# Layer A of a two-layer encoder trunk: tokens transposed before their norm, and the second half of the queries made tile by tile

## The chip, the cores and the metric

One core of a Trainium2 chip runs the whole kernel in one launch. The metric is device time in microseconds (us) of one execution; lower is better. Inputs and output are float32.

## The reference, cut to what matters

The input x has 512 tokens of 1024 values. There are two residual layers, A and B, each followed by an MLP with a squared ReLU. The change lies in layer A, the sparse attention:

```
xn = x * rsqrt(mean(x * x) + EPS) * g_attn_a
q, k, v, qi, ki, wi = split(xn @ w_in)          # 1024, 256, 256, 512, 64, 8 columns
q, k, qi, ki = rope(q), rope(k), rope(qi), rope(ki)
wi = wi * (8 ** -0.5 * 64 ** -0.5)
score[t, s] = sum_h relu(qi[t, h] . ki[s]) * wi[t, h]   # allowed keys only
keep the 128 best keys of each query
o = softmax(q . k / 8 over the kept keys) @ v     # 16 heads, 4 key heads
h = x + o @ w_o
```

The rotation (rope) multiplies pairs of columns by cos and sin of the position, so it is linear in its input; v and wi are linear in xn as well.

## The kernel before, in words

Tokens are worked on in four tiles t of 128. A product in float32 is made of three matmuls: each operand is split into a high part (a cast, on ACT) and a low part (the rest, on DVE or by a POOL-issued accumulating DMA), and high*high, high*low and low*high are added up in a PSUM bank (mm3). wunit loads a piece of weights (raw) and makes its two parts (whi, wlo).

A planner sets the order. The body only records operations; schedule (L237) then simulates the five queues with a cost per operation, gives each operation a due time from the sum of PE costs before it in program order, and picks for each engine the most urgent one that is ready and whose tiles have room. emit writes the instructions out in that order, and on the chip each engine runs its own list strictly in that order. Nearly all instructions therefore carry the helper's line, L416, in the profile, and are told apart by the names of their tiles. Tiles live in slots by size: 41 slots of 1024 words per partition (L423). Weight pieces may be fetched up to 40 us of PE cost ahead, and split up to 30 us ahead (L422). PSUM has 8 banks.

Layer A runs so. x is loaded by tiles (L601). rstd (L562) makes the norm factor r of a tile: two Square pieces on ACT with a sum, then small steps on DVE and ACT. The gain g_attn_a is loaded as one row (grow, L607) and spread over 128 partitions by two float32 matmuls of a row of ones (tile g). norm_T (L584) makes y = x * r * g on DVE, transposes y on PE (tile yT) and splits the result into xT. The planner has 20 transposes of the identity (tile warm) at the start of PE's list.

Then come the products with pieces of w_in: for every tile t, 264 columns (idx2: part of qi, ki, wi) and 320 columns (idx1: the rest of qi), with the index scores (tile ix) behind them; then keys and values by tokprod (kvdone, L736); then the queries in two halves hb of 512 columns. tokprod (L527) in order "k" takes one weight piece for all four tiles before the next piece, with four banks open. After each product, rope (L636) does three multiplications on DVE with the tables cosT and sinT and an add on POOL, and for queries stacks (L658) transposes the result (tile qT) and splits it into the stacks qs[t][hb].

The attention takes tile t after tile t, and for each of the four key heads: products lg of queries and keys, a sum with the mask on DVE, exp on ACT, scaling on POOL, transposes pT, and products pv. Key heads 0 and 1 use the first half of the queries, 2 and 3 the second. topk(t) makes the mask of tile t on DVE, in 16 rounds; topk(1) is recorded before tile 0, topk(2) and topk(3) behind tiles 0 and 1. The output projection (products tp on oT) follows, then the MLP, which begins with the products up. A later helper, column (L1008), loads the gains of layer B, gq and gkv, with a transposing DMA of single values.

Of the kernel before, what the change touches and what calls it, by code (L numbers as in the profile page):

```python
# [429 lines left out]
def body(ctx, tc, a, out):  # L430
# [25 lines left out]
    def const(shape, name):  # L456
        return rec.tile(VPool(rcst, name, 1), shape, F32, name)
# [10 lines left out]
    def bank(shape, name):  # L468
        return rec.tile(p_ps, shape, F32, name, quotas.get(name))
# [27 lines left out]
    def lows(stage):  # L497
        lo_eng[0] = G if stage in CFG["dl"] else V
# [58 lines left out]
    def gain(row):  # L557
        g = rec.tile(p_bt, [128, D], F32, "g")
        SP.dma_start(g, bass.AP(tensor=row.tensor, offset=row.offset, ap=[[0, 128], [1, D]]))
        return g  # L560

    def rstd(src, cuts=(0, 512, D)):  # L562
        n = len(cuts) - 1
        ss = small(n, "ss")
        for i in range(n):
            c = slice(cuts[i], cuts[i + 1])
            S.activation(scr([128, cuts[i + 1] - cuts[i]], "junk"), src[:, c], AF.Square, accum_out=ss[:, i:i + 1])
        v = small(4, "v")
        for i in range(1, n):
            V.tensor_tensor(v[:, 0:1], v[:, 0:1] if i > 1 else ss[:, 0:1], ss[:, i:i + 1], op=OP.add)  # L570
        V.tensor_scalar(v[:, 0:1], v[:, 0:1], 1.0 / D, EPS, op0=OP.mult, op1=OP.add)
        S.activation(v[:, 1:2], v[:, 0:1], AF.Ln)
        S.activation(v[:, 1:2], v[:, 1:2], AF.Exp, scale=-0.5)
        V.scalar_tensor_tensor(v[:, 2:3], v[:, 1:2], v[:, 0:1], v[:, 1:2], op0=OP.mult, op1=OP.mult)
        V.tensor_scalar(v[:, 2:3], v[:, 2:3], -0.5, 1.5, op0=OP.mult, op1=OP.add)
        r = small(1, "r")
        V.tensor_tensor(r, v[:, 1:2], v[:, 2:3], op=OP.mult)
        return r
# [5 lines left out]
    def norm_T(src, r, g, xT, t):  # L584
        for i in range(2):
            y = scr([128, 512], "y")
            c = slice(512 * i, 512 * i + 512)
            gc = g[i] if isinstance(g, list) else g[:, c]
            V.scalar_tensor_tensor(y, src[:, c], r, gc, op0=OP.mult, op1=OP.mult)
            b = bank([128, 4, 128], "yT")  # L590
            for k in range(4):
                PE.transpose(b[:, k, :], y[:, 128 * k:128 * k + 128], ident)
            c = slice(128 * t, 128 * t + 128)
            for k in range(2):
                split(xT[0][2 * i + k][:, :, c], xT[1][2 * i + k][:, :, c], b[:, 2 * k:2 * k + 2, :])

    def xl(xT):
        return lambda k, t: tuple(x[k // 2][:, k % 2, 128 * t:128 * t + 128] for x in xT)
# [5 lines left out]
        return x  # L604

    xt = [xload(0)]
    grow = const([1, D], "grow")  # L607
    SP.dma_start(grow, a["g_attn_a"][0:1])
    ones = const([1, 128], "ones")
    V.memset(ones, 1.0)  # L610
    g = [bank([128, 512], "g") for _ in range(2)]
    for i in range(2):
        PE.matmul(g[i], ones, grow[:, 512 * i:512 * i + 512], start=True, stop=True)

    wb = bank([128, 128], "warm")
    for _ in range(CFG["warm"]):
        PE.transpose(wb, ident, ident)

    w_in = a["w_in_a"][0]
    xT = new_xT()  # L620
    norm_T(xt[0], rstd(xt[0]), g, xT, 0)
    lows("i2")
    ui2 = [wN(w_in, 256 * j, 1856, 264) for j in range(4)]
    xt.append(xload(1))
    norm_T(xt[1], rstd(xt[1]), g, xT, 1)
    SP.dma_start(cosT, a["cos"].rearrange("(t p) d -> p t d", p=128))
    SP.dma_start(sinT, a["sin"].rearrange("(t p) d -> p t d", p=128))
    lows("i1")
    ui1 = [wN(w_in, 256 * j, 1536, 320) for j in range(4)]
    lows("a")  # L630
    for t in (2, 3):
        xt.append(xload(t))
        norm_T(xt[t], rstd(xt[t]), g, xT, t)
    SP.dma_start(bfc, a["b_f"].rearrange("(h o) -> h o", o=1))

    def rope(dst, src, t, nh, dup=None):  # L636
# [36 lines left out]
    def idx2(t, b):  # L673
        q = scr([128, 512], "qr")
        qr[t] = q
        if t:
            S.activation(wi[:, t, :], b[:, 256:264], AF.Copy, scale=float(8 ** -0.5 * 64 ** -0.5))
        k2 = scr([128, 1, 2, 64], "k2")
        if t:
            rope(q[:, 0:192].heads(64), b[:, 0:192].heads(64), t, 3)  # L680
        rope(q[:, None, 192:256], b[:, None, 192:256], t, 1, dup=k2)
        kb = bank([128, 128], "kb")
        PE.transpose(kb, k2.flat(), ident)
        c = slice(128 * t, 128 * t + 128)
        split(kid[:, 0, c], kid[:, 1, c], kb)
# [50 lines left out]
    def kvdone(t, b):  # L736
        ka, k = scr([128, 4, 64], "ka"), scr([128, 4, 2, 64], "kr")
        rope(ka, b[:, 0:256].heads(64), t, 4, dup=k)
        for c, e in ((0, 64), (64, 320)):
            S.copy(vf[t][:, c:e], b[:, 256:256 + e - c])  # L740
        if vv is not None:
            v = vv[t // 2][:, t % 2]
            split(v[:, :, 0, :], v[:, :, 1, :], b[:, 256:512].heads(64))
        krs[t] = k

    tokprod(xl(xT), w_in, 0, 8, 1024, 512, kvdone)
# [4 lines left out]
        split(kd[n][:, 0, :], kd[n][:, 1, :], b.flat())  # L751

    qs = [[big([128, 2, 4, 128], "qs") for _ in range(2)] for _ in range(NT)]
    for hb in range(2):
        def qdone(t, b, hb=hb):
            q = scr([128, 512], "qr")
            rope(q.heads(64), b.heads(64), t, 8)
            stacks(qs[t][hb], q, 0.125)
        tokprod(xl(xT), w_in, 0, 8, 512 * hb, 512, qdone)


    def topk(t):
# [7 lines left out]

    oT = new_xT("oT")
    topk(1)
    for t in range(NT):
        n = 128 * (t + 1)
        for kv in range(4):
            st = small(4, "st")
            rc = small(4, "rc")
            Ps = []
            for h in range(4):
                b = bank([128, 512], "lg")  # L780
                for p in range(2):
                    PE.matmul(b[:, :n], qs[t][kv // 2][:, h % 2, 2 * (kv % 2) + h // 2, :], kd[kv][:, p, :n],
                              start=p == 0, stop=p == 1)
                l = scr([128, 512], "l")
                mn = small(1, "mn")
                V.tensor_tensor_reduce(out=l[:, :n], in0=b[:, :n], in1=masks[t], op0=OP.add, op1=OP.min,
                                       scale=-1.0, scalar=BIG, accum_out=mn)
                S.activation(l[:, :n], l[:, :n], AF.Exp, bias=mn, scale=-1.0, accum_out=st[:, h:h + 1])
                Ps.append(l)
            V.reciprocal(rc, st)  # L790
            for h in range(4):
                G.tensor_scalar(Ps[h][:, :n], Ps[h][:, :n], rc[:, h:h + 1], 0.0, op0=OP.mult, op1=OP.add)
            pt = []
            for j in range(t + 1):
                b = bank([128, 4, 128], "pT")
                for h in range(4):
                    PE.transpose(b[:, h, :], Ps[h][:, 128 * j:128 * j + 128], ident)
                if t in CFG["pvf"]:
                    pf = scr([128, 4, 128], "pf")
                    S.copy(pf, b)  # L800
                    pt.append(pf)
                else:
                    ph, pl = scr([128, 4, 128], "ph", F32R), scr([128, 4, 128], "pl", F32R)
                    split(ph, pl, b)
                    pt.append((ph, pl))
            c = slice(128 * t, 128 * t + 128)
            if t in CFG["pvf"]:

                o = bank([128, 2, 128], "pv")
                for e in (1, 0):  # L810
                    for j in range(t + 1):
                        PE.matmul(o if e else o[0:64], vf[j][:, 64 * kv + 64 - 64 * e:64 * kv + 128],
                                  pt[j][:, e:4:2, :], start=j == 0, stop=j == t)
            else:

                pv, u, o = bank([128, 4, 128], "pv"), scr([64, 4, 128], "u"), scr([128, 2, 128], "o")
                for j in range(t + 1):
                    for i in range(2):
                        PE.matmul(pv, vv[j // 2][:, j % 2, kv].flat(), pt[j][i], start=j + i == 0, stop=j == t and i == 1)
                S.copy(u, pv[64:128])  # L820
                for e in range(2):
                    V.tensor_tensor(o[64 * e:64 * e + 64], pv[0:64, e:4:2, :], u[:, e:4:2, :], op=OP.add)
            split(oT[0][kv][:, :, c], oT[1][kv][:, :, c], o)
        if t in (0, 1):
            topk(t + 2)
# [179 lines left out]


    hd = rec.tile(p_dr["hd"], [T, D], F32, "hd")
    def column(row, name):  # L1008

        g = const([128, 8], name)  # L1010
        SP.dma_start(g, row)
        return g

    gq = column(a["g_attn_b"][0].rearrange("(k p) -> p k", p=128), "gq")
    gkv = column(a["g_kv"].rearrange("(k p) -> p k", p=128), "gkv")
    xq, xk = new_xT(), new_xT()

    def afterA(t):
# [276 lines left out]
```

## Time and profile before

| | us |
|---|---|
| three runs | 1181.00 (median), 1179.83 to 1181.45 |
| the profiled execution: its own time | 1181.78 |
| the profiled execution: its span, first to last instruction | 1179.7 |
| PE busy in the span | 1154.7 (98%) |
| DVE, ACT, POOL busy | 773.3, 737.5, 235.4 |

The trace has one execution. PE is TensorE, DVE VectorE, ACT ScalarE, POOL GpSimd, SP the engine that issues most transfers; PEld is the weight load of PE. A stretch is counted in us from the start of the span. The granted clock (PEclk) is the share of TensorE's full speed that the throttle let through: 1.00 stands for 2.4 GHz, 0.50 for 1.2 GHz. A group's row gives the count, the busy time and the mean duration of one instruction in ns. Matmuls overlap, so the pace of a run of matmuls is its length divided by its count and not their mean duration.

### The profile page before, as it was taken

Reading aid. Unit: us, or ns where it says so; the run is one execution under the profiler, and the core shown is the slowest. Engines: PE = TensorE matmul, PEld = TensorE weight load, DVE = VectorE, ACT = ScalarE, POOL = GpSimd, SP = SyncE. Lnnn points to the kernel's source line nnn. Section 1 sums busy time; section 2 is a strip of 40 time slices with the busy share of each in tenths; the row PEclk is TensorE's granted clock in tenths of the full one; section 3 lists DMA queues with packets and bytes.
Section 4 is the critical chain, followed back from the end, with each engine's and each line's share of the span. In section 5 each row is a group of like instructions: output and inputs, shape, how many; then the busy total and the mean of one; then the engine's idle time right before and its main releaser. Section 6 shows DMA issues by size and latency. Waiting matters only on the chain. (4 is left out here: it accounts for less than half of the span.)

```text
span 1179.7 us, 16374 instructions
## 1 busy us (share of the span) xinstructions
PE 1154.7 (98%) x5688; PEld 959.0 (81%) x5688; DVE 773.3 (66%) x1474; ACT 737.5 (63%) x1385; POOL 235.4 (20%) x391
## 2 busy tenths in 40 slices
PE   8999899999999999999999999999999999999997
PEld 7878677888888888888897878888888888888885
DVE  6799979365735836658665458874558358366496
ACT  7751499955745745658584148997558456555562
POOL 0311344310110100200111058972101001002001
PEclk9999799999999999999999999999999999999999
DMA  9941620873791981965886313588638919729601
GB/s 296 223 90 63 206 55 19 179 176 129 191 272 39 247 248 57 248 215 140 235 199 143 108 37 108 167 209 175 160 113 214 250 56 234 244 71 244 220 18 72
DMA packets 147349, 187.85 MB, mean 159 GB/s; under 512 B 10162, under 2 KB 94130, under 8 KB 147267
## 3 DMA queue, kind: packets, MB, share of 16 engines
q1 hardware_dynamic: 131714, 130.18, 35.1%
q0 software_dynamic: 15552, 56.63, 24.8%
q8 instruction: 45, 0.74, 0.3%
q14 instruction: 38, 0.30, 0.1%
HBM read 125.94 MB, written 4.23 MB: 110 GB/s over the span
## 5 line engine op out<-in xcount | busy, mean ns | idle before, releaser
L416 PE MATMUL up<-xT,whi 128*128 128x512 f32 (+1 forms) x1152 | 323.4, 366 | 0.0
L416 PEld LDWEIGHTS up<-xT,whi 128*128 128x128 f32 x1152 | 207.9, 189 | 34.8
L416 POOL DMA_DIRECT2D wlo<-raw x108 | 95.3, 883 | 702.1 <-ACT wlo L416 291.7
L416 DVE TENSOR_TENSOR dlo<-raw,dhi 128x1024 fp32r<-128x1024 f32 x112 | 136.3, 1226 | 143.4 <-ACT dhi L416 89.3
L416 PE MATMUL up<-xT,wlo 128*128 128x512 f32 (+1 forms) x576 | 210.0, 366 | 0.0
L416 PE MATMUL tp<-dhi,xhi 128*128 128x512 f32 (+1 forms) x452 | 171.8, 389 | 1.2 <-DVE h L416 0.8
L416 PE MATMUL tp<-dlo,xhi 128*128 128x512 f32 (+1 forms) x452 | 171.5, 387 | 0.0
L416 PE MATMUL tp<-dhi,xlo 128*128 128x512 f32 (+1 forms) x452 | 170.8, 388 | 0.0
L416 ACT CAST whi<-raw 128x1024 fp32r<-128x1024 f32 (+2 forms) x124 | 124.2, 1025 | 74.2 <-DMA raw<-in_w_up_dram 66.3
L416 ACT CAST dhi<-raw 128x1024 fp32r<-128x1024 f32 x112 | 116.5, 1047 | 66.3 <-PE up L416 64.1
L416 ACT ACTIVATE wlo<-whi 128x1024 fp32r<-128x1024 f32 x108 | 112.7, 1061 | 23.9 <-DMA wlo<-raw 10.6
L416 PE MATMUL tp<-whi,xT 128*128 128x512 f32 (+2 forms) x432 | 123.5, 372 | 0.0
L416 PEld LDWEIGHTS up<-xT,wlo 128*128 128x128 f32 x576 | 108.4, 189 | 17.5
L416 DVE TENSOR_TENSOR h<-tp,h 128x512 f32<-128x512 f32 (+1 forms) x97 | 64.6, 681 | 80.8 <-PE tp L416 80.7
L416 PEld LDWEIGHTS tp<-dhi,xhi 128*128 128x128 f32 x452 | 84.8, 188 | 21.5 <-DVE h L416 1.4
L416 PEld LDWEIGHTS tp<-dhi,xlo 128*128 128x128 f32 x452 | 84.7, 188 | 17.4
L416 PEld LDWEIGHTS tp<-dlo,xhi 128*128 128x128 f32 x452 | 84.9, 188 | 16.9
L416 DVE TENSOR_TENSOR raw<-raw 128x1024 f32<-128x1024 f32 x64 | 76.6, 1220 | 19.3 <-DMA raw<-in_w_down_dram 18.7
L416 PEld LDWEIGHTS tp<-whi,xT 128*128 128x128 f32 x432 | 78.8, 192 | 12.2 <-ACT xT L416 0.2
L416 ACT ACTIVATE r<-up 128x512 f32<-128x512 f32 x64 | 37.9, 592 | 79.6 <-PE up L416 79.6
L416 ACT ACTIVATE l<-l,mn 128x128 f32<-128x128 f32 (+3 forms) x128 | 71.5, 563 | 22.4 <-DVE mn L416 22.0
L416 POOL TENSOR_SCALAR l<-l,rc 128x128 f32<-128x128 f32 (+3 forms) x128 | 69.1, 561 | 59.4 <-DVE rc L416 42.5
(178 smaller groups left out, 1939.6 us busy)
## 6 DMA issues: line engine op xcount, KB each, us to landing
wlo<-raw POOLq DMA_DIRECT2D x108, 512.0 KB, 8.6
raw<-in_w_down_dram SPq DMA_DIRECT2D x96, 512.0 KB, 11.5
raw<-in_w_up_dram SPq DMA_DIRECT2D x64, 512.0 KB, 6.7
raw<-in_w_kv_b_dram SPq DMA_DIRECT2D x16, 512.0 KB, 5.6
raw<-in_w_in_a_dram SPq DMA_DIRECT2D x12, 512.0 KB, 6.5
raw<-in_w_o_a_dram SPq DMA_DIRECT2D x8, 512.0 KB, 4.8
raw<-in_w_q_b_dram SPq DMA_DIRECT2D x8, 512.0 KB, 7.2
ck<-cd SPq DMA_DIRECT2D x16, 256.0 KB, 3.7
```

What stands on the lines that cost most here:

```text
L416: getattr(self.engs[o.eng], o.fn)(*a, **k)
```

## The change

The tokens are transposed as they are loaded. The gain g_attn_a becomes a column of 8 values per partition (column, now with a load of 8 rows, a transpose on PE and a copy on ACT), and is applied as the scale of the split into xT. The norm factor r is kept in a small table rs[t]; factor(t) multiplies it into the rows of cosT and sinT of that tile, so that the rotation applies it to queries and keys; values and the index weights wi take it as the scale of their copies. Tiles 0 and 1 are transposed each by itself, with splits 128 wide; tiles 2 and 3 together, 256 wide.

Both halves of the query weights are now recorded ahead of the query products. These run by token tile: first half for all tiles, second half of tile 0, then the second half of tile t + 1 at the head of attention tile t. The gains of layer B are loaded by the new column as well.

```diff
--- before.py
+++ after.py
@@ -559,6 +559,14 @@
         SP.dma_start(g, bass.AP(tensor=row.tensor, offset=row.offset, ap=[[0, 128], [1, D]]))
         return g
 
+    def column(g, name):
+
+        rows, b, c = const([8, 128], name + "r"), bank([128, 8], "gc"), const([128, 8], name)
+        SP.dma_start(rows, g.rearrange("(k p) -> k p", p=128))
+        PE.transpose(b, rows, ident[0:8, 0:8])
+        S.copy(c, b)
+        return c
+
     def rstd(src, cuts=(0, 512, D)):
         n = len(cuts) - 1
         ss = small(n, "ss")
@@ -585,8 +593,7 @@
         for i in range(2):
             y = scr([128, 512], "y")
             c = slice(512 * i, 512 * i + 512)
-            gc = g[i] if isinstance(g, list) else g[:, c]
-            V.scalar_tensor_tensor(y, src[:, c], r, gc, op0=OP.mult, op1=OP.mult)
+            V.scalar_tensor_tensor(y, src[:, c], r, g[:, c], op0=OP.mult, op1=OP.mult)
             b = bank([128, 4, 128], "yT")
             for k in range(4):
                 PE.transpose(b[:, k, :], y[:, 128 * k:128 * k + 128], ident)
@@ -604,33 +611,55 @@
         return x
 
     xt = [xload(0)]
-    grow = const([1, D], "grow")
-    SP.dma_start(grow, a["g_attn_a"][0:1])
-    ones = const([1, 128], "ones")
-    V.memset(ones, 1.0)
-    g = [bank([128, 512], "g") for _ in range(2)]
-    for i in range(2):
-        PE.matmul(g[i], ones, grow[:, 512 * i:512 * i + 512], start=True, stop=True)
+    ga = column(a["g_attn_a"][0], "ga")
 
     wb = bank([128, 128], "warm")
     for _ in range(CFG["warm"]):
         PE.transpose(wb, ident, ident)
 
+
+
     w_in = a["w_in_a"][0]
     xT = new_xT()
-    norm_T(xt[0], rstd(xt[0]), g, xT, 0)
+    rs = {}
+
+    def x_T(ts):
+        n = len(ts)
+        c = slice(128 * ts[0], 128 * ts[-1] + 128)
+        for k in range(0, 8, 4 // n):
+            b = bank([128, 4 // n, 128 * n], "yT")
+            for i in range(4 // n):
+                for u, t in enumerate(ts):
+                    PE.transpose(b[:, i, 128 * u:128 * u + 128], xt[t][:, 128 * (k + i):128 * (k + i) + 128], ident)
+            for i in range(k, k + 4 // n):
+                split(xT[0][i // 2][:, i % 2, c], xT[1][i // 2][:, i % 2, c], b[:, i - k, :], scale=ga[:, i:i + 1])
+
+    def factor(t):
+        r = const([128, 2], "ra%d" % t)
+        rr = rstd(xt[t])
+        V.tensor_copy(r[:, 0:1], rr)
+        V.tensor_scalar(r[:, 1:2], rr, float(8 ** -0.5 * 64 ** -0.5), None, op0=OP.mult)
+        rs[t] = r
+        V.tensor_scalar(cosT[:, t, :], cosT[:, t, :], r[:, 0:1], None, op0=OP.mult)
+        V.tensor_scalar(sinT[:, t, :], sinT[:, t, :], r[:, 0:1], None, op0=OP.mult)
+
+    x_T((0,))
     lows("i2")
     ui2 = [wN(w_in, 256 * j, 1856, 264) for j in range(4)]
     xt.append(xload(1))
-    norm_T(xt[1], rstd(xt[1]), g, xT, 1)
     SP.dma_start(cosT, a["cos"].rearrange("(t p) d -> p t d", p=128))
     SP.dma_start(sinT, a["sin"].rearrange("(t p) d -> p t d", p=128))
+    factor(0)
+    x_T((1,))
+    factor(1)
     lows("i1")
     ui1 = [wN(w_in, 256 * j, 1536, 320) for j in range(4)]
     lows("a")
     for t in (2, 3):
         xt.append(xload(t))
-        norm_T(xt[t], rstd(xt[t]), g, xT, t)
+    x_T((2, 3))
+    factor(2)
+    factor(3)
     SP.dma_start(bfc, a["b_f"].rearrange("(h o) -> h o", o=1))
 
     def rope(dst, src, t, nh, dup=None):
@@ -674,7 +703,7 @@
         q = scr([128, 512], "qr")
         qr[t] = q
         if t:
-            S.activation(wi[:, t, :], b[:, 256:264], AF.Copy, scale=float(8 ** -0.5 * 64 ** -0.5))
+            S.activation(wi[:, t, :], b[:, 256:264], AF.Copy, scale=rs[t][:, 1:2])
         k2 = scr([128, 1, 2, 64], "k2")
         if t:
             rope(q[:, 0:192].heads(64), b[:, 0:192].heads(64), t, 3)
@@ -737,10 +766,10 @@
         ka, k = scr([128, 4, 64], "ka"), scr([128, 4, 2, 64], "kr")
         rope(ka, b[:, 0:256].heads(64), t, 4, dup=k)
         for c, e in ((0, 64), (64, 320)):
-            S.copy(vf[t][:, c:e], b[:, 256:256 + e - c])
+            S.activation(vf[t][:, c:e], b[:, 256:256 + e - c], AF.Copy, scale=rs[t][:, 0:1])
         if vv is not None:
             v = vv[t // 2][:, t % 2]
-            split(v[:, :, 0, :], v[:, :, 1, :], b[:, 256:512].heads(64))
+            split(v[:, :, 0, :], v[:, :, 1, :], b[:, 256:512].heads(64), scale=rs[t][:, 0:1])
         krs[t] = k
 
     tokprod(xl(xT), w_in, 0, 8, 1024, 512, kvdone)
@@ -751,12 +780,23 @@
         split(kd[n][:, 0, :], kd[n][:, 1, :], b.flat())
 
     qs = [[big([128, 2, 4, 128], "qs") for _ in range(2)] for _ in range(NT)]
-    for hb in range(2):
-        def qdone(t, b, hb=hb):
+
+    def qdone(hb):
+        def done(t, b):
             q = scr([128, 512], "qr")
             rope(q.heads(64), b.heads(64), t, 8)
             stacks(qs[t][hb], q, 0.125)
-        tokprod(xl(xT), w_in, 0, 8, 512 * hb, 512, qdone)
+        return done
+    uq = [[wN(w_in, 256 * j, 512 * hb, 512) for j in range(4)] for hb in range(2)]
+
+    def qprod(hb, t):
+        b = bank([128, 512], "tp")
+        for k in range(8):
+            mm3(b, xl(xT)(k, t), tuple(u[:, k % 2, :] for u in uq[hb][k // 2]), k == 0, k == 7)
+        qdone(hb)(t, b)
+
+    for t in range(NT):
+        qprod(0, t)
 
 
     def topk(t):
@@ -770,8 +810,11 @@
 
     oT = new_xT("oT")
     topk(1)
+    qprod(1, 0)
     for t in range(NT):
         n = 128 * (t + 1)
+        if t + 1 < NT:
+            qprod(1, t + 1)
         for kv in range(4):
             st = small(4, "st")
             rc = small(4, "rc")
@@ -1005,14 +1048,8 @@
 
 
     hd = rec.tile(p_dr["hd"], [T, D], F32, "hd")
-    def column(row, name):
-
-        g = const([128, 8], name)
-        SP.dma_start(g, row)
-        return g
-
-    gq = column(a["g_attn_b"][0].rearrange("(k p) -> p k", p=128), "gq")
-    gkv = column(a["g_kv"].rearrange("(k p) -> p k", p=128), "gkv")
+    gq = column(a["g_attn_b"][0], "gq")
+    gkv = column(a["g_kv"], "gkv")
     xq, xk = new_xT(), new_xT()
 
     def afterA(t):
```

## Rows read from the trace of the kernel before

**Rows 1.** The page: span, and busy time, share and instructions of PE.

```profile
span 1179.7 us, 16374 instructions
PE 1154.7 (98%) x5688; PEld 959.0 (81%) x5688; DVE 773.3 (66%) x1474; ACT 737.5 (63%) x1385; POOL 235.4 (20%) x391
```

**Rows 2.** Stretches: PE, PEld, DVE, ACT, POOL busy (count); clock; DMA share, GB/s.

```profile
217.00:252.00 35.00, 35.00 (x164) 28.54 (x162) 14.91 (x38) 25.07 (x48) 7.52 (x9) 1.00 0.81 169
...
600.00:1179.70 579.70, 566.39 (x2778) 471.87 (x2776) 359.94 (x616) 353.69 (x654) 132.14 (x243) 0.99 0.57 151
```

**Rows 3.** Timeline of the start: start us, us, engine, what, count.

```profile
2.90 6.96 SPq L416 DMA_DIRECT2D raw<-in_w_in_a_dram  x8
...
12.02 0.63 ACT L416 CAST whi<-raw 128x528 fp32r<-128x528 f32 x1
...
12.86 0.74 PE L416 MATMUL tp<-whi,xT 128*128 128x264 f32 x2
...
16.51 2.56 DVE L416 TENSOR_TENSOR wlo<-raw,whi 128x528 fp32r<-128x528 f32 x4
...
16.75 0.54 PE L416 MATMUL tp<-whi,xT 128*128 128x320 f32 x1
```

**Rows 4.** Stretches of the start.

```profile
13.60:16.70 3.10, 1.24 (x8) 0.84 (x8) 3.10 (x10) 3.10 (x10) 0.00 (x0) 1.00 1.16 315
16.70:20.10 3.40, 3.37 (x15) 3.06 (x15) 3.40 (x7) 2.80 (x6) 0.00 (x0) 0.52 1.04 383
20.10:32.20 12.10, 11.91 (x89) 11.46 (x88) 10.05 (x29) 9.38 (x16) 3.82 (x6) 0.99 0.97 252
```

**Rows 5.** Forms, ACT and DVE to 60 us; last row ACT, 126 to 218.

```profile
L416 ACT CAST xT<-yT 128x256 fp32r<-128x256 f32 x16 | 5.6, 385 | 2.5 <-PE yT L416 1.9 <-DVE xT L416 0.6
L416 ACT ACTIVATE junk<-x 128x512 f32<-128x512 f32 x8 | 5.0, 622 | 3.3 <-DMA x<-in_x_dram 3.2
...
L416 ACT CAST kid<-kb 128x128 fp32r<-128x128 f32 x3 | 0.8, 272 | 0.0
...
L416 DVE TENSOR_TENSOR xT<-yT,xT 128x256 fp32r<-128x256 f32 x16 | 6.0, 418 | 1.4 <-ACT xT L416 1.4
L416 DVE SCALAR_TENSOR_TENSOR y<-x,r,g 128x512 f32<-128x512 f32 x8 | 5.9, 743 | 0.4 <-PE g L416 0.2
...
L416 DVE TENSOR_TENSOR kid<-kb,kid 128x128 fp32r<-128x128 f32 x3 | 0.9, 288 | 2.1 <-ACT kid L416 2.1
...
L416 ACT ACTIVATE l<-l,mn 128x128 f32<-128x128 f32 x16 | 6.4, 398 | 21.8 <-DVE mn L416 21.6
```

**Rows 6.** Stretches from the top-k to the end of the attention.

```profile
50.00:104.00 54.00, 53.51 (x245) 42.50 (x243) 53.51 (x154) 24.21 (x50) 8.12 (x10) 1.00 0.47 111
104.00:126.40 22.40, 22.13 (x104) 18.36 (x105) 21.88 (x48) 3.83 (x7) 2.77 (x3) 1.00 0.42 142
126.40:133.00 6.60, 3.69 (x28) 3.08 (x26) 6.55 (x22) 3.06 (x8) 5.04 (x4) 0.99 1.07 301
133.00:146.40 13.40, 11.79 (x46) 9.40 (x46) 11.64 (x47) 10.81 (x39) 4.28 (x13) 0.50 0.26 85
146.40:157.00 10.60, 10.42 (x58) 6.55 (x57) 9.63 (x41) 9.37 (x34) 5.09 (x12) 0.99 0.18 54
...
166.00:217.00 51.00, 50.74 (x278) 40.58 (x277) 42.96 (x115) 50.13 (x114) 23.57 (x37) 1.00 0.24 48
```

**Rows 7.** Waits, 126 to 147 us: who for whom, us, times, longest.

```profile
POOL qr L416 <- DVE rtmp L416: 20.7, 4, 19.7
...
PE qT L416 <- POOL qr L416: 3.0, 4, 1.0
```

**Rows 8.** DMA issues to 30 us: first weight pieces, count, KB, us to landing.

```profile
raw<-in_w_in_a_dram SPq DMA_DIRECT2D x4, 264.0 KB, 7.7
```

**Rows 9.** Stretches, PE's instructions on oT alone: busy (count), clock, DMA.

```profile
166.00:200.00 34.00, 6.92 (x18) 1.00 0.13 25
200.00:217.00 17.00, 9.86 (x31) 1.00 0.45 96
```

## The prediction

> **What bounds the kernel now.** I read the page first: PE is busy 1154.7 of 1179.7 us [rows 1]. With an engine at 98% nothing but PE's own lost time can be won, so I looked for where it is lost, in two forms: idle time, and time at a low granted clock, which the busy column hides. The view of busy time by stretch shows both. From 217 to 252 us, in the output projection, PE is never idle. After 600 us it is idle 579.7 - 566.4 = 13.3 us, in stages that the diff touches only with two small gain columns [rows 2]. So the question is what is lost before 217 us. There are two places.
>
> The start. PE's first two products issue at 12.86 us, and the run of products that doesn't stop again begins at 16.75 us [rows 3]. Between 13.6 and 16.7 PE works 1.24 of 3.10 us, and the next 3.4 us are granted 0.52, nearly all at 1.2 GHz [rows 4]. DVE and ACT are full in both stretches. The reader should see the order on DVE: eight y = x*r*g of 743 ns and sixteen xT low parts of 418 ns [rows 5] stand ahead of the wlo casts, which come at 16.51 us [rows 3].
>
> The first attention tile. Until 126.4 us PE is dense. Then it works 3.69 of 6.60 us, and after that the clock is granted 0.50 for 13.4 us [rows 6]. What PE waits for is in the list of waits: the query transposes wait for POOL's rotation add, four waits, and POOL's add waits in turn for DVE's part of the rotation [rows 7]. DVE is busy 53.5 of 54.0 us before 104 us and 21.88 of 22.40 us after it [rows 6], with the top-k rounds of the code between everything else. So PE runs out of independent products exactly when the latency chain of tile 0 begins.
>
> **Part 1, tokens transposed unnormed.** Taken away: the two gain broadcasts (four PE records, before any product), y on DVE (8 x 743 ns = 5.9 us [rows 5]), and above all the wait of every transpose for the norm factor. The Square pieces (8 x 622 ns = 5.0 us of ACT [rows 5]) and the small steps behind them now have one kind of reader, the rotation tables and value scales, which are needed only when a product is done.
>
> Added on ACT and DVE: tiles 0 and 1 are split in 128-wide pieces, 16 on each engine, tiles 2 and 3 in eight 256-wide ones, all with a pointer scale. No row has this form. On ACT a 128-wide piece lies between 272 ns (an unscaled cast, kid) and 398 ns (exp with a pointer bias); I take the middle, 0.33, and add the same 0.06 to the 256-wide 0.385: 16 x 0.33 + 8 x 0.45 = 8.9 us against 16 x 0.385 = 6.2, so +2.7 us [rows 5] (+1.2 at the lower end, 16 x 0.272 + 8 x 0.385 = 7.4; +4.4 with 398 ns and 0.53). On DVE likewise 16 x 0.35 + 8 x 0.48 = 9.4 against 16 x 0.418 = 6.7, +2.7 us. The factor steps on DVE are four per tile; I take 0.2 us each, under the 288 ns of a 128-wide PSUM read, 3.2 us. DVE comes out even: -5.9 + 2.7 + 3.2 = 0. The three column copies on ACT (at most 0.3 each) are nothing beside that; gq and gkv lie hundreds of us ahead of their use, and their new transposes are two of PE's 5688 records [rows 1].
> The Trainium skill's page "Perfetto Trace Analysis" (Optimizing Scalar/DVE Operations) speaks against small pieces: each instruction pays a fixed access overhead, about 51 ns on ACT and 125 ns on DVE from PSUM. By its figures the eight extra pieces would be an estimated 0.4 us on ACT and 1.0 us on DVE. The rows give 2 x 0.272 - 0.385 = 0.16 and 2 x 0.288 - 0.418 = 0.16 us per extra piece, 1.3 us on each; my sum uses the rows.
>
> What it gives PE: the first weight piece is issued at 2.90 us and lands 7.7 us later (the median of the four) [rows 3, 8], with a cast of 0.63 us [rows 3] that is 11.2 us. With nothing else ahead, products could run from 11.2 instead of 16.75 us: 5.5 us is the upper end. The slow stretch moves with them rather than vanishing, since PE again pauses between transposes and first products. I subtract 0.6 us for three products that were already done before 16.75, and about 1 us for the extra ACT work while ACT is the fullest engine (3.10 of 3.10 us [rows 4]): **4 us**. The other end is a loss: if products still wait until 16.75 us and ACT's 2.7 us come in front of its casts, -2.7. The lead then has to survive DVE's full stretch. DVE idled 12.1 - 10.05 = 2.1 us between 20.1 and 32.2 [rows 4], behind PE and ACT, so its start moves with PE's; I cost that at nothing.
>
> **Part 2, the second half of the queries by tile.** No work is added: 96 products of 512 columns in another order. At PE's rate (104 records in 22.13 us [rows 6], 0.21 each) one tile is 24 x 0.21 = 5.1 us. Tiles 0 and 1 still go ahead of the attention by program order; tiles 2 and 3, 10 us, are free to stand in the gaps of attention tile 0. What is lost there now: 6.60 - 3.69 = 2.9 us idle, 13.40 - 11.79 = 1.6 us idle, and half of 11.79 = 5.9 us to the clock [rows 6], 10.4 us together. That is the upper end; the lower is 0. Ten us of filler against 4.5 us idle is enough, and where PE was dense in [rows 6] it was granted 1.00, which is 2.4 GHz, but the pieces don't fit every pause, and POOL's rotation add now stands between the attention's scalings. I take **8 us**. Attention tile 1 needs no filler: from 146.4 to 157 PE is busy 10.42 of 10.60 us [rows 6].
>
> Queues it moves past: SP's four loads of the second half are issued no later than now; behind them stand the output weights, their accumulating DMAs on POOL, and the h loads. PE has first use of the output weights at 166 us, and only 6.92 + 9.86 us of that work before 217 us [rows 9]; then come 35 us with nothing but that, so nothing there is urgent unless the rival below holds. ACT and DVE do the same work as before from 104 us on; ACT is nearly full from 166 to 217 (50.13 of 51 [rows 6]), and starting tile 0 some 10 to 20 us earlier gives it room.
>
> **The sum.** Against the profiled execution's own 1181.8 us: 1181.8 - 4 - 8 = 1169.8. That execution is 0.8 us above the median of the runs shown, so for a median: 1181.0 - 12 = **1169.0**.
>
> **The rivals.**
> B, the gap stays. DVE is full from 50 us on, and the filler's rotations and stacks are DVE's work too. If tile 0's chain, not PE's lack of products, sets its length, PE drains the filler and then waits as before. Only part 1 is left: 1181.0 - 4 = 1177.0. It is also what comes if the planner puts all four tiles ahead of the attention, and so the change doesn't do what it says. Against it: the waits name the rotation of the last products, which is now done tiles earlier.
> C, the lead of the start is eaten by ACT, the fullest engine there, which got 2.7 us more. Part 2 alone: 1181.0 - 8 = 1173.0.
> D, the slower side: tile memory. There are 41 slots of 1024 words. Now xT (8) and the second half's weights (8) must be held into the attention beside keys (4), values (2), oT (8) and five to six query stacks, 35 to 36 slots; an output weight piece takes three. If these weights come so late that none of their products runs before the attention ends, PE loses the 6.92 + 9.86 us that now stand there [rows 9]; in records this is 49 x 0.21 = 10.3 us. A second slow stretch like that at 133 us costs 5.9 more [rows 6]. Net, with both gains kept: -12 + 10.3 + 5.9 = +4.2, 1185.2. It decides if the last tile of the second half ends later than some 20 us before attention tile 2 runs dry. Against it: tile 3's products have priority over attention tile 2, and free 16 slots at once.
> The Trainium skill's "Perfetto Trace Analysis" (Optimization Strategy) says that the same gap repeating on an engine that should be saturated can mean too little memory for the next tile; by that rule D is the outcome. The trace of before shows no such gap from 166 to 217 us (50.74 of 51), and no run here shows it yet.
>
> **Chances.** Forecast (both parts, 7 to 15.5 us) 0.56; B 0.14; C 0.14; D 0.16. What a measurement of this kernel can tell from no change is about 0.2%, 2.4 us: 1178.6 to 1183.4. C and the forecast are faster; of B 0.08 is, the rest is within; of D 0.13 is slower and 0.03 within. Faster 0.78, same 0.09, slower 0.13. The range takes the forecast with both upper ends (1181.0 - 5.5 - 10.4 = 1165.1, and half a us for the replanned stages behind), C, and B's better half: 1164.5 to 1179.5.
>
> **What would show it.** Part 1 right: x transposed before 10 us, the run of products from about 11.5 to 12.5 us, no y before the output projection. Part 2 right: attention's first lg some 10 to 20 us before 126 us, products on xT between them to 130 us or later, granted clock 1.00 from 126 to 147 us, and the up product, now at the end of the 217 to 252 stretch, starting near 240 us. B shows as PE idle beside DVE at 100%; C as ACT full and PE waiting for a cast between 12 and 20 us; D as SP waiting for slots and no oT product before the attention ends. A clock granted 0.50 anywhere between 100 and 217 us would prove the 8 us wrong.

## The result, and the profile after

Four runs after: 1168.49 us median (1168.06 to 1169.15). The kernel before, on the same chip: 1181.22 (1179.83 to 1181.82). The ratio is 0.9894 with an interval of [0.9877, 0.9911], 12.5 us less by the ratio and 12.7 by the medians. The forecast was 1169.0. The profiled execution took 1168.06 us.

The page of the kernel after answers to [rows 1]: the span is 13.5 us shorter, PE's busy time 12.9 us shorter, with one record less. So what went is mostly time in which PE was *busy*, not time in which it was idle.

```profile
span 1166.2 us, 16382 instructions
...
PE 1141.8 (98%) x5687; PEld 948.6 (81%) x5687; DVE 771.8 (66%) x1489; ACT 741.6 (64%) x1396; POOL 236.5 (20%) x391
```

Busy time by stretch of the kernel after, with the columns of [rows 2]. The first three rows answer to [rows 4], the others to [rows 6].

```profile
13.60:16.70 3.10, 3.10 (x27) 3.10 (x27) 2.57 (x7) 3.10 (x12) 0.00 (x0) 1.00 1.16 313
16.70:20.10 3.40, 3.40 (x27) 3.30 (x26) 3.37 (x13) 3.40 (x8) 0.00 (x0) 1.00 1.05 386
20.10:32.20 12.10, 10.33 (x76) 9.91 (x75) 11.22 (x47) 7.96 (x20) 3.76 (x5) 1.00 1.06 379
...
50.00:104.00 54.00, 52.19 (x244) 41.61 (x243) 53.08 (x140) 28.45 (x53) 10.07 (x11) 1.00 0.48 107
104.00:126.40 22.40, 21.77 (x120) 17.26 (x119) 22.18 (x80) 11.49 (x40) 8.12 (x15) 1.00 0.01 2
126.40:133.00 6.60, 6.60 (x35) 4.19 (x34) 6.51 (x24) 4.01 (x15) 2.72 (x6) 1.00 0.00 1
133.00:146.40 13.40, 13.39 (x81) 10.47 (x82) 12.76 (x45) 11.43 (x34) 5.53 (x12) 1.00 0.78 236
...
166.00:217.00 51.00, 50.97 (x269) 40.86 (x268) 35.95 (x86) 50.63 (x102) 22.26 (x33) 1.00 0.41 84
```

Three things are to be seen. From 126.4 to 146.4 us PE worked 15.48 of 20.00 us before, with 0.50 granted in the last 13.4 us; now it works 19.99 at 1.00. From 13.6 to 20.1 it worked 4.61 of 6.50 us, with 0.52 granted in the last 3.4 us; now all of it at 1.00. And from 20.1 to 32.2 and from 50 to 104 PE is idle 1.77 and 1.81 us, where it was idle 0.19 and 0.49: something is given back there.

The order around the attention, one row for each tile's products on PE in the kernel after (count, duration in ns, first and last start in us):

```profile
L416 PE MATMUL tp<-whi,xT x304: 279/389/504, 12.5 to 151.3; 128*128 128x512 f32 x96, 128*128 128x264 f32 x36, 128*128 128x320 f32 x20
...
L416 PE MATMUL lg<-kd,qs x128: 220/338/487, 113.6 to 188.7; 128*128 128x128 f32 x32, 128*128 128x256 f32 x32, 128*128 128x384 f32 x32, 128*128 128x512 f32 x32
...
L416 PE MATMUL up<-xT,whi x192: 277/283/397, 240.3 to 285.6; 128*128 128x256 f32 x128, 128*128 128x512 f32 x64
```

The attention starts 12.8 us earlier (126.4 before), the last product on xT stands 37.7 us inside it, at 151.3 us (at its very start before, 126.5), and the first up comes 12.3 us earlier (252.6 before). In the stretch up to the first up, PE is idle 252.60 - 241.49 = 11.1 us before and 240.30 - 229.76 = 10.5 us after; so 11.7 of the 12.3 us are busy time: the two slow stretches, and at the start the products of g and the slow transposes.

First starts and median time, in us, of the kernels that the next section speaks of:

| | before | part 1 alone | part 2 alone | both |
|---|---|---|---|---|
| first index score (ix) | 39.5 | 35.8 | 39.4 | 35.3 |
| first lg | 126.4 | 121.3 | 117.2 | 113.6 |
| first up | 252.6 | 248.3 | 244.9 | 240.3 |
| median time | 1181.2 | 1176.4 | 1173.1 | 1168.5 |

### The profile page after: what moved, and what is told of

It reads as the page before. It is cut to its first block, busy times and chain, and to the rows that moved or that the text cites. A ratio compares the mean times of both kernels' runs of the same rounds, so it can differ in the third digit from the quotient of the medians.

```text
span 1166.2 us, 16382 instructions
## 1 busy us (share of the span) xinstructions
PE 1141.8 (98%) x5687; PEld 948.6 (81%) x5687; DVE 771.8 (66%) x1489; ACT 741.6 (64%) x1396; POOL 236.5 (20%) x391
## 5 line engine op out<-in xcount | busy, mean ns | idle before, releaser
L416 ACT ACTIVATE wlo<-whi 128x1024 fp32r<-128x1024 f32 x108 | 112.4, 1059 | 20.8 <-DMA wlo<-raw 10.3
L416 PE MATMUL tp<-wlo,xT 128*128 128x512 f32 (+2 forms) x216 | 78.4, 372 | 0.5 <-DVE ra L416 0.5
## 6 DMA issues: line engine op xcount, KB each, us to landing
raw<-in_w_down_dram SPq DMA_DIRECT2D x96, 512.0 KB, 10.9
```

What stands on the lines that cost most here:

```text
L416: getattr(self.engs[o.eng], o.fn)(*a, **k)
```

## The experiments

**The two parts, each alone.** In the kernel after, the query products and the attention's loop were put back as before:

```diff
+    for hb in range(2):
+        def qdone(t, b, hb=hb):
...
+        tokprod(xl(xT), w_in, 0, 8, 512 * hb, 512, qdone)
...
-    qprod(1, 0)
...
-        if t + 1 < NT:
-            qprod(1, t + 1)
```

> The changed kernel with both query halves made as before, by tokprod ahead of the attention. Theory (the two parts add up): about 3 to 4.5 us under the kernel before, 1176.7 to 1178.2, with the stretch granted 0.50 at attention tile 0 still there. Rival (the lead of the start is swallowed by the DVE-bound stretch): 1180 to 1182. Rival (part 1 carries most of the 12.7): under 1174.

Measured: 1176.39 us (1176.1 to 1177.18) against 1180.78 for the kernel before, ratio 0.9967 [0.9954, 0.998], 3.9 us less. The stretches of the first attention tile are as in [rows 6]:

```profile
126.40:133.00 6.60, 5.13 (x23) 4.51 (x23) 6.29 (x20) 6.35 (x18) 2.97 (x6) 0.50 0.50 179
133.00:146.40 13.40, 13.40 (x61) 9.75 (x60) 11.04 (x53) 9.76 (x39) 4.53 (x13) 0.65 0.20 65
```

The other half: the kernel before, with the query part of the diff and nothing else of it.

```diff
+    for t in range(NT):
+        qprod(0, t)
...
+    qprod(1, 0)
     for t in range(NT):
         n = 128 * (t + 1)
+        if t + 1 < NT:
+            qprod(1, t + 1)
```

> The kernel before with the second query half by token tile between the attention tiles. Theory (the parts add up): 8 to 9.5 us under the kernel before, 1171.7 to 1173.2, granted clock 1.00 from 105 to 215 us, first products still at 16.7 us. Rival (the interleaving only works with the earlier start): over 1176.

Measured: 1173.09 us (1171.99 to 1174.5), ratio 0.9934 [0.9918, 0.9951], 7.8 us less. The slow stretch is gone with this part alone:

```profile
126.40:133.00 6.60, 6.60 (x39) 4.54 (x37) 6.54 (x28) 5.26 (x21) 4.22 (x12) 1.00 0.00 0
133.00:146.40 13.40, 13.40 (x80) 9.76 (x79) 13.01 (x51) 11.92 (x37) 6.82 (x13) 1.00 0.38 123
```

3.9 + 7.8 = 11.7 us by the ratios, with the two together 12.5; by the medians 4.4 + 7.7 = 12.1 and 12.7. The parts add up within the intervals. The table shows where each has its gain: part 1 has 3.7 us at the first index score and keeps it; part 2 has nothing there, 9.2 us at the first lg and 7.7 us at the first up.

**Order by tile, or products between the attention tiles?** Part 2 does both. Here the second half stays by token tile, but all four tiles go ahead of the attention:

```diff
-    qprod(1, 0)
+    for t in range(NT):
+        qprod(1, t)
     for t in range(NT):
         n = 128 * (t + 1)
-        if t + 1 < NT:
-            qprod(1, t + 1)
```

> The changed kernel with all four tiles of the second query half ahead of the attention, still tile by tile. Theory (only products that stand between attention tiles fill the gap): the gain of part 2 is gone, 1175.5 to 1177.5, as with part 1 alone, and a stretch granted 0.50 is back near attention tile 0. Rival (the order by token tile, which finishes the first tiles earlier, is what counts): 1168 to 1171.

Measured: 1177.76 us (1176.49 to 1178.32), ratio 0.9967 [0.9956, 0.9979], the same as part 1 alone. The order by tile alone is worth nothing; what counts is that PE has products that need no attention result while the attention's first chain runs. Without them the pause is back, with a wait of 2.4 us of lg for the last rotation on DVE. The stretch and the wait:

```profile
126.40:166.00 39.60, 36.78 (x201) 28.66 (x200) 32.59 (x133) 34.19 (x107) 18.09 (x39) 0.87 0.56 167
```

```profile
PE lg L416 <- DVE rtmp L416: 2.4, 1, 2.4
```

In the same 39.6 us the kernel before works 34.89 us at 0.83, the kernel after 39.31 at 1.00.

**What part 1 consists of: the products of g.** The kernel before, with the gain spread over the partitions by a DMA in place of the float32 matmuls:

```diff
-    g = [bank([128, 512], "g") for _ in range(2)]
-    for i in range(2):
-        PE.matmul(g[i], ones, grow[:, 512 * i:512 * i + 512], start=True, stop=True)
+    g = gain(a["g_attn_a"][0])
```

> The kernel before with the gain spread over the partitions by a broadcasting transfer in place of the two float32 products. Theory (these products keep PE at half pace): transposes at 0.11 us from the start, products at full pace, 1 to 3 us under the kernel before, 1178.2 to 1180.2. Rival: no difference, 1180.5 to 1182, with products from 16.7 to 20.1 us still granted 0.5.

Measured: 1179.52 us (1179.01 to 1181.18), ratio 0.9994 [0.9985, 1.0004], no difference shown, and at most 1.8 us. The transposes are still slow (1.97 / 8 = 0.25 us each), as the rival had it; but the median lies in the theory's range, and from 16.7 to 20.1 us the clock granted was 1.00, as the theory had it. The run can't settle it, for the transfer that stands in for the products brings a delay of its own. PE is free at 5.9 us and then waits 5.15 us for y; y waits for the gain g until 10.24 us, where it started at 8.00 in the kernel before.

```profile
3.76 2.13 PE L416 MATMUL warm<-ident 128*128 128x128 f32 x9
...
10.24 2.08 DVE L416 SCALAR_TENSOR_TENSOR y<-x,r,g 128x512 f32<-128x512 f32 x3 [0.21 <-DMA g<-in_g_attn_a_dram]
...
11.04 1.97 PE L416 MATMUL yT<-ident,y 128*128 128x128 f32 x8 [5.15 <-DVE y L416]
```

And the other way: the kernel after, with those products put back. Their result is not read; the output does not depend on them.

```diff
     ga = column(a["g_attn_a"][0], "ga")
+    grow = rec.tile(p_bt, [1, D], F32, "grow")
+    SP.dma_start(grow, a["g_attn_a"][0:1])
...
+    for i in range(2):
+        PE.matmul(g[i], ones, grow[:, 512 * i:512 * i + 512], start=True, stop=True)
```

> The changed kernel with the two float32 products of a row of ones and the gain row put back at the start; nothing reads them. Theory (what brought full pace at the start is that PE has no pause of over two us between the identity transposes and the first products; these products only fill time in which PE waits for x and weights): within 1 us of the changed kernel, 1167.5 to 1169.5, transposes of x still near 0.12 us each. Rival (these products themselves keep PE at half pace): 1170 to 1172.5, transposes at 0.22 us and products from 13 us on at half pace.

Measured: 1171.36 us (1171.06 to 1172.81), ratio 0.9916 [0.9901, 0.993], 2.6 to 2.9 us above the kernel after in its two sets of runs (1168.79 in the second, below). PE's list is worked off in order, so the transposes of x stand behind them:

```profile
3.82 3.76 PE L416 MATMUL g<-grow,ones 1*128 1x512 f32 x4
7.50 1.11 PE L416 MATMUL yT<-ident,x 128*128 128x128 f32 x4
...
13.84 3.75 PE L416 MATMUL yT<-ident,x 128*128 128x128 f32 x18
17.34 0.37 PE L416 MATMUL tp<-whi,xT 128*128 128x264 f32 x1
```

The transposes start 2.3 us later than in the kernel after and take 3.75 / 18 = 0.21 us each instead of 2.18 / 18 = 0.12; the first product comes at 17.34 us instead of 12.46, and the first ix at 39.0 instead of 35.3. From 17.34 us on the products run at full pace, so the rival had the time and the transposes right, not the pace of the products. So the four records cost some 2.7 us in the kernel after, where PE no longer waits for y behind them. What they cost in the kernel before stays open. The theory is answered too: with them, PE had no longer pause between the identity transposes and the first products than without them, and the transposes of x were slow all the same.

**The gain columns of layer B.** In the kernel after, gq and gkv were loaded again by a transposing DMA of single values:

```diff
-    gq = column(a["g_attn_b"][0], "gq")
-    gkv = column(a["g_kv"], "gkv")
+    gq = column4(a["g_attn_b"][0].rearrange("(k p) -> p k", p=128), "gq")
+    gkv = column4(a["g_kv"].rearrange("(k p) -> p k", p=128), "gkv")
```

> The changed kernel with the gains of layer B loaded by single values again, 1024 of 4 bytes each, as before the change. Theory (no one on PE's path waits for what they delay): within 0.8 us of the changed kernel, 1167.7 to 1169.3, with two us near 21 us in which the transfers move under 170 GB/s. Rival (they hold up the key and value weights): 1 to 3 us slower, 1169.5 to 1171.5.

Measured: 1167.19 us (1166.9 to 1167.7), ratio 0.9878 [0.9864, 0.9893]. The transfers do fall, to 72 and 52 GB/s from 21 to 23 us, but the time does not suffer. The new column brings nothing there; if anything it costs some 1 us: all four runs lie under all eight of the kernel after, but the intervals of the ratios overlap, and the difference is not traced.

**The kernel after once more**, unchanged.

> The changed kernel once more, as the reference on this chip for the two runs beside it. Expected as before: 1167.5 to 1169.5, ratio 0.988 to 0.991.

Measured: 1168.79 us (1167.76 to 1169.06), ratio 0.9897 [0.9882, 0.9912]. Its profile turned out to be an experiment of its own. The start of this execution, by stretch:

```profile
13.60:16.70 3.10, 2.78 (x13) 2.78 (x14) 2.70 (x7) 3.10 (x11) 0.00 (x0) 0.59 1.15 314
16.70:20.10 3.40, 3.40 (x27) 3.40 (x26) 3.22 (x12) 3.40 (x9) 0.00 (x0) 0.87 1.06 387
20.10:32.20 12.10, 12.10 (x92) 12.10 (x91) 10.73 (x48) 8.76 (x22) 3.74 (x5) 1.00 1.06 384
```

The same program was granted 0.59 and 0.87 here and 1.00 in the first profile, where it then idled 1.77 us between 20.1 and 32.2. The first index score comes at 35.2 us here and at 35.3 there. So the faster pace of the first products was lost again before that. Where, is seen at tile k, the last add of the index key's rotation, which is on DVE (those of the queries are on POOL). First the kernel after in the first profile:

```profile
26.45 0.28 DVE L416 TENSOR_TENSOR k<-qr,rtmp 128x128 f32<-128x128 f32 x1
...
27.85 0.89 POOL L416 TENSOR_TENSOR qr<-qr,rtmp 128x192 f32<-128x192 f32 x1
...
28.39 1.20 POOL L416 DMA_DIRECT2D wlo<-raw  x1
28.39 2.24 DVE L416 TENSOR_TENSOR k<-qr,rtmp 128x128 f32<-128x128 f32 x1
...
29.01 1.47 POOL L416 TENSOR_TENSOR qi<-qi,rtmp 128x320 f32<-128x320 f32 x1
29.85 0.99 POOL L416 TENSOR_SCALAR qi<-qr 128x192 f32<-128x192 f32 x1
...
30.78 0.30 PE L416 MATMUL kb<-ident,k 128*128 128x128 f32 x1 [1.47 <-DVE k L416]
```

Then the second profile of it:

```profile
29.22 0.95 DVE L416 TENSOR_TENSOR k<-qr,rtmp 128x128 f32<-128x128 f32 x1
...
30.05 1.48 POOL L416 TENSOR_TENSOR qi<-qi,rtmp 128x320 f32<-128x320 f32 x1
...
30.67 0.27 PE L416 MATMUL kb<-ident,k 128*128 128x128 f32 x1
```

With POOL idle k takes 0.28 us. In the first profile it starts 0.83 us earlier, with the faster clock, but takes 2.24 us beside POOL's work; in the second it takes 0.95. It ends at 30.63 and 30.17 us. In the first profile PE waits 1.47 us for it and starts kb at 30.78; in the second PE comes to kb without a wait, at 30.67, held up by its own slower products. So the two come out alike.

k ends just after an add of POOL does: 0.15 us after the 320-wide one in the first profile (30.48), 0.40 us after the 192-wide one in the second (29.77). POOL itself is not slowed. Its rows overlap one another; counted from the end of the row before, the 320-wide add takes 0.89 us and the copy 0.36, against 0.87 and 0.35 for the same instructions elsewhere in the kernel. Which of POOL's instructions holds k, and why it was over sooner in the second profile, is not shown. The Trainium skill has the rule in "SBUF — State Buffer" (Who interferes with whom): a DVE instruction with two SBUF inputs contends with a GpSimd instruction that reads SBUF. k is of that kind, and these rows agree.

**Is tile memory at its edge?** The kernel after with 36 slots of 1024 words in place of 41, as a test of rival D:

```diff
-    "slots": {1024: 41, 512: 18, 256: 7, 128: 8, 64: 1}, ...
+    "slots": {1024: 36, 512: 18, 256: 7, 128: 8, 64: 1}, ...
```

> The changed kernel with 36 instead of 41 slots of 1024 words, five fewer than it has; the work is the same. Theory (memory is near its limit in the attention, as in rival D of the prediction, but 41 slots are enough): clearly slower, 4 to 12 us over the changed kernel, 1172 to 1180, with PE idle or a lower granted clock between attention tile 0 and the output projection. Rival (slots don't matter there): within 1.5 us, 1167 to 1170.

Measured: 1189.59 us (1187.83 to 1190.67), ratio 1.0062 [1.0046, 1.0079], 21 us above the kernel after, more than the 4 to 12 expected. But the first up comes only 6.5 us later (246.8); the rest is lost behind it, as here between the first up and the start of layer B, where the kernel after works 339.46 of the 340 us:

```profile
260.00:600.00 340.00, 335.35 (x1573) 279.24 (x1572) 211.02 (x272) 203.92 (x321) 26.17 (x30) 1.00 0.69 182
```

This alone can't tell whether the change needs the slots or the program does. So the same edit was made in the kernel before.

> Control for the run with 36 slots: the kernel before with 36 instead of 41 slots of 1024 words. Theory (the loss there is the whole program's need of memory, most of it in the MLPs and layer B, and the change adds only a part): 10 to 18 us slower than the kernel before, 1191 to 1199, so that the change is still worth 5 to 12 us at 36 slots. Rival D (the loss was the change's own, from what it holds in the attention): under 4 us slower than before, 1181 to 1185.

Measured: 1200.68 us (1199.08 to 1203.67), ratio 1.0172 [1.0154, 1.019], 19.7 us more. The slots are the whole program's need: by the medians the change is worth 11.1 us with 36 of them and 12.7 with 41, by the ratios 13.0 and 12.5.

**A later place for the second half.** Tile t + 1 of the second half is recorded between key heads 1 and 2 of attention tile t and not at its head; gq and gkv as single values.

```diff
-        if t + 1 < NT:
-            qprod(1, t + 1)
         for kv in range(4):
+            if kv == 2 and t + 1 < NT:
+                qprod(1, t + 1)
```

> The changed kernel with the gains of layer B loaded by single values, and with the second query half of tile t + 1 recorded before key head 2 of attention tile t instead of at its head. Theory (PE is already dense from 104 us to the end of the attention, so a better place for the filler has nothing left to win): within 1 us of the changed kernel, 1167 to 1169.5. Rival (tile 0 starts earlier and the output projection gains): 1164 to 1166.

Measured: 1167.4 us (1167.27 to 1169.32), ratio 0.9891 [0.9876, 0.9905], the same as with the single values alone (1167.19). The attention starts at 107.1 us instead of 113.6, the up products at 239.5 instead of 240.3. The exact place doesn't matter, and an earlier start of the attention is no gain by itself: PE is full either way.

**POOL's copy moved away from DVE's k.** On top of that kernel, the copy of 192 index-query columns goes to ACT:

```diff
-        G.tensor_scalar(q[:, 320:512], qr[t][:, 0:192], 1.0, 0.0, op0=OP.mult, op1=OP.add)
+        S.copy(q[:, 320:512], qr[t][:, 0:192])
```

> The run beside it with one more edit: the 192-column copy of the index query moves from POOL to ACT. Theory (near 29 us DVE's add k takes 2.2 us instead of 0.28 because POOL works beside it, and PE waits 1.5 us for it; with one POOL operation less behind it the wait is shorter): 0.5 to 1.5 us under the run beside it, first index product before 35 us. Rival (the next wait in the chain of DVE and ACT takes its place): no difference.

Measured: 1165.54 us (1165.25 to 1165.9), ratio 0.9871 [0.9855, 0.9888]: the fastest of all, its slowest run 1.4 us under the fastest of the kernel that it was made from. So the edit wins some 2 us. Its profile was granted 1.00 from 13.6 us on, like the first one of the kernel after, so the two can be laid side by side:

```profile
28.64 0.38 DVE L416 TENSOR_TENSOR k<-qr,rtmp 128x128 f32<-128x128 f32 x1
```

```profile
20.10:32.20 12.10, 11.74 (x89) 11.44 (x88) 10.13 (x49) 8.76 (x23) 4.13 (x5) 1.00 0.88 256
```

k ends at 29.02 us and not at 30.63, PE works 11.74 of 12.10 us and not 10.33, and the first index score comes at 34.0 and not at 35.3.

That the gain comes from k beside POOL is not shown by this. In the profile of the kernel that it was made from, which was granted 0.60 from 13.6 to 16.7 us, k was over at 30.21 us, before POOL's copy even began (30.94):

```profile
29.25 0.96 DVE L416 TENSOR_TENSOR k<-qr,rtmp 128x128 f32<-128x128 f32 x1
```

Against that profile the first index score is 1.2 us earlier, the first lg 1.8 (105.3) and the first up 2.4 (237.1). The start of the clock is not the reason either: a run of that kernel with a mean clock of 0.999 took 1167.29 us. The planner orders the whole program anew with the copy on ACT, and which of the moved instructions gives the gain stays open.

## Why the prediction was right, and where it was off

**Right, by its own steps.** Part 1 was put at 4 us and is 3.9; part 2 at 8 and is 7.8; they add. The signs it named are there: the first lg 12.8 us earlier (10 to 20 named), products on xT to 151.3 us (130 or later), clock 1.00 through 126 to 147 us, the up product at 240.3 (near 240), no y ahead of the output projection. One is missed by a little: the transposes of x end at 10.9 us, where "before 10" was named. The reading behind part 2, that PE had run out of independent products just when the first chain began, is shown from both sides: part 2 alone removes the slow stretch, and the second half by tile, but ahead of the attention, brings it back.

**Rivals.** B, the gap stays, is what the kernel with all four tiles ahead does (1177.8, where B said 1177.0); the change itself has the products in the gap. C, the lead eaten by ACT, fell with part 1 alone at 1176.4. D, tile memory, is right in that memory is near its edge, some 20 us for five slots, but that holds alike before and after. The change has its products on oT from 155.0 us on, long before the attention's last lg at 188.7, and from 166 to 217 us PE works 50.97 of 51.00 us:

```profile
L416 PE MATMUL tp<-whi,oT x128: 387/389/483, 155.0 to 238.8; 128*128 128x512 f32 x128
```

The rule that spoke for D, in "Perfetto Trace Analysis" of the Trainium skill (Optimization Strategy), goes by a gap that repeats. The change shows none there, and the stretch shown above of the kernel with 36 slots is no clear case either: 3.53 of its 4.65 us idle lie in one place, from 580 to 600 us.

**Off: when the products start.** The step "with nothing else ahead, products could run from 11.2" had a condition that didn't hold. They start at 12.46, and without a pause from 13.33. PE's and ACT's timelines of the kernel after:

```profile
8.71 2.18 PE L416 MATMUL yT<-ident,x 128*128 128x128 f32 x18 [0.63 <-DVE xT L416]
...
12.46 0.19 PEld L416 LDWEIGHTS tp<-whi,xT 128*128 128x128 f32 x1 [1.81 <-ACT whi L416]
12.46 0.39 PE L416 MATMUL tp<-whi,xT 128*128 128x264 f32 x1 [1.57 <-DVE r L416]
...
13.33 0.39 PE L416 MATMUL tp<-wlo,xT 128*128 128x264 f32 x1 [0.48 <-DVE ra L416]
```

```profile
8.16 0.62 ACT L416 ACTIVATE junk<-x 128x512 f32<-128x512 f32 x1
...
9.95 0.64 ACT L416 ACTIVATE junk<-x 128x512 f32<-128x512 f32 x1
...
11.75 1.73 ACT L416 CAST whi<-raw 128x528 fp32r<-128x528 f32 x3
```

PE's first wait is put down to DVE's r, which this product doesn't read, but its weight load's to ACT's whi: the first of the three casts begins at 11.75 us and ends 0.67 us later, as the product issues. Ahead of it on ACT stand two Square pieces that nothing needed yet. The prediction took 1 us off for ACT's fullness, and the sum held by that, in part by luck (below).

**Off: the slow stretch at the start.** It was to "move with them rather than vanish", and in the first profile it vanished. That this changed nothing (35.2 and 35.3 us in two profiles of one program) leads to the weakest step: DVE's "start moves with PE's; I cost that at nothing". In the first profile DVE bounds this stretch, through k beside POOL, and in the kernel before k took 2.50 us as well:

```profile
31.15 2.50 DVE L416 TENSOR_TENSOR k<-qr,rtmp 128x128 f32<-128x128 f32 x1
```

DVE's busy share, from which the prediction read two us of room [rows 4], counts such a stretch as work. In sum, by the first profile: 16.75 - 13.33 = 3.4 us earlier, 3.4 x (1 - 0.52) = 1.6 us by the full clock, 11.91 - 10.33 = 1.6 us given back. 3.4 us are left, close to the 3.7 at the first index score of part 1 alone. So the 4 us came out partly by luck: the lead of the products was 2.1 us shorter than the 5.5 taken, which the 1.6 us taken off it for other reasons nearly made up.

**Off: what part 1 consists of.** The "four PE records, before any product" stood without a price. With y gone they cost some 2.7 us, most of the 3.9; what their removal is worth without that of y is open, since the kernel before without g has the late gain in it.

**Off: why part 2 is 8 us and not 10.4.** The reason given was that "the pieces don't fit every pause". They do: with part 2 alone PE works all of the 20 us from 126.4 to 146.4 at 1.00. Most of what is missing is given back in other stretches: this kernel idles 1.37 us from 50 to 104 us and 1.21 from 157 to 166, where the kernel before idled 0.49 and nothing. So the 8 us, chosen and not worked out, were right for another reason.

**Sizes.** The split pieces, in the kernel after to 35 us:

```profile
L416 ACT ACTIVATE xT<-yT,ga 128x128 fp32r<-128x128 f32 x16 | 5.6, 382 | 0.7 <-PE yT L416 0.6
L416 ACT ACTIVATE junk<-x 128x512 f32<-128x512 f32 x8 | 5.1, 653 | 0.8 <-DMA x<-in_x_dram 0.8
L416 ACT ACTIVATE xT<-yT,ga 128x256 fp32r<-128x256 f32 x8 | 3.6, 518 | 0.0
```

```profile
L416 DVE SCALAR_TENSOR_TENSOR xT<-yT,ga,xT 128x128 fp32r<-128x128 f32 x16 | 5.3, 347 | 6.5 <-PE yT L416 5.7 <-ACT xT L416 0.7
L416 DVE SCALAR_TENSOR_TENSOR xT<-yT,ga,xT 128x256 fp32r<-128x256 f32 x8 | 3.6, 476 | 0.5 <-ACT xT L416 0.5
```

On DVE 0.35 and 0.48 us, as taken. On ACT 0.382 and 0.518 where 0.33 and 0.45 were taken, so 16 x 0.382 + 8 x 0.518 = 10.3 us, 4.1 more than before instead of 2.7. An extra piece costs 2 x 0.382 - 0.518 = 0.25 us on ACT and 0.22 on DVE; the rows of before gave 0.16, and the Trainium skill's "Perfetto Trace Analysis" (Optimizing Scalar/DVE Operations) 0.051 and 0.125: both too low, the page on ACT by a factor of five.

## What to carry to other kernels

Ask what an engine at 98% does in the stretch where it has nothing independent to do: here 4.5 us of idle time cost another 5.9 in slow clock, and ten us of products moved there won most of both, while their order alone won nothing. Put a price on each step ahead of the first product: four records without one cost 2.7 us once the wait for y was gone. Undo the parts one by one in both kernels, and look at what the stand-in of a part taken out does: a late transfer hid the answer in one of them. When a busy engine bounds a stretch, look at the longest duration of each instruction against its shortest, since a stretched instruction shows as work.

## What the runs showed of the hardware

An add of two SBUF tiles on DVE, 128 x 128, took 0.28 us with POOL idle. Beside POOL's adds it took 0.38, 0.95, 0.96, 2.24 and 2.50 us in five of the profiles, up to nine times as long, and ended 0.15 to 0.40 us after one of these adds did. The adds were not slowed (0.89 us against 0.87).

The granted clock was 1.00 in two places that differ in pace: 16 transposes of the kernel before took 3.62 us, 0.23 each, in the stretch from 9.4 to 13.6 us, and 18 of the kernel after 2.18 us, 0.12 each, between 8.7 and 10.9. The kernel after with g put back read 1.00 too, with transposes of 0.21 us. Without g, the kernel before had 0.51 in the first of these stretches, with transposes of 1.97 / 8 = 0.25 us. So at the start of a program the pace of equal instructions is the surer sign, and the column is to be read beside it.

One program was granted 1.00 in one execution and 0.59 in another between 13.6 and 16.7 us. In the second its first six transposes of x took 1.49 us instead of 0.90, both from 5.23 us on, with the same products ahead of them. What decides that wasn't found; it moved neither the first index score nor the first up (240.3 and 240.1).
